# Low parts of two token tiles on GpSimd, and router and gather work at a higher priority, in a hybrid trunk layer with 32 experts

## The chip, the cores and the metric

The kernel runs on one core of one Trainium2 chip. The metric is the device time of one execution in microseconds (us), as the median of several runs.

## What is computed

One layer over 512 latent tokens of 1024 channels, with a context of 256 tokens. Three token mixers (centred pooling, differential attention, a bidirectional RWKV scan) are merged and projected back to 1024 channels, and the result is added to the tokens. Then comes a mixture of experts, which is what this case is about: each token chooses one of 4 groups and in it 2 of 8 experts. Cut to that part:

```python
lg  = h @ w_rg                                   # h: modulated RMSNorm of the tokens, 512 x 1024
grp = argmax(lg)                                 # 1 of 4 groups
le  = (h @ w_re) of that group                   # 8 experts of it
top_v, top_i = lax.top_k(le, 2)
gates = softmax(lg)[grp] * softmax(top_v)
eid   = grp * 8 + top_i                          # 32 experts in all
y_e   = (silu(xb @ w_g[e]) * (xb @ w_u[e])) @ w_d[e]     # 1024 -> 512 -> 1024, tokens of expert e
out   = x + mod[5] * sum over the two experts of gate * y_e
```

The weights of the 32 experts are 201 MB in fp32, and each is used once.

## The kernel before

**Stages.** The mixers and the merge take the first part of the execution. Then the output projection is made in four column blocks of 256, each for four token tiles of 128 (`out_mm` L1446 on TensorE, `out_add` L1452 to L1458 on VectorE and ScalarE). As soon as a tile has its last block, its routing begins. The experts follow, each for at most 64 tokens (a path for more is not taken here). The experts come in batches of four, whose tokens are gathered together.

**Routing of one tile t** (all of it stands between the last output products and the first expert). `turned` transposes the tile's tokens on TensorE (L1369), and ScalarE copies them (L1370). `logits` multiplies them by the router's weights (L1376, 8 products a tile, 32 in all). `route` (L1380 to L1401, all on VectorE but for one power on GpSimd, L104) scales them, takes the largest group and the two largest experts and writes one-hot rows. `count` (L1409, and L1410 on VectorE) numbers the tokens of every expert, which gives each token a slot. `normed` writes the normalised tokens twice over. The high part is a rounded copy (L1436, ScalarE, in two halves). The low part is what the rounding left out (L1437, VectorE, 128x1024). A plain copy (L1440, ScalarE) goes to memory (L1441). High and low part together are multiplied as two products where fp32 would be needed.

**Gathering the first batch.** `chosen` (L1500, VectorE) makes a 0/1 matrix of a tile's tokens against the 256 slots of four experts. `rows_of` (L1506, TensorE) multiplies high and low part by it, summed over the four tiles, and `put` (L1511 on ScalarE, L1513 on VectorE) writes the result to xT, the input of the first four experts. `slots` (L1484 to L1491) gathers the gates (`gates`, L1416 to L1427, put into `tgx` by L1601 to L1603). Later batches are fetched from the stored copy instead.

**Experts.** `up` (L1608) makes the first expert product from xT and the weights, `hidden` and `turn_` the activation, `down` (L1643) the second product, and `parts_of` (L1661, GpSimd) and `add` (L1653) bring it to the tokens. `load` (L1257) issues the weights' transfers on SyncE, 1 MB at a time, into a ring of 13 buffers (`ew`), and two more loads go into buffers that the stage needs later anyway (names `oh`, `yhl`, `xT`). Several of the ring's buffers lie where the mixers and the routing kept their data, so a load waits until those have been read. One of them (buffer 10) lies where the plain copies, named F, were.

**Order.** The code is written tile by tile, and a scheduler sets each engine's order by a priority that falls with the place in the code. `tc.high_priority(n)` moves what it encloses ahead by n places. Each engine then works through its list in order, and each instruction waits for the semaphores of what it needs. In names of the trace, `xn` is the tokens' high and low parts, `oh` the 0/1 matrices, `F` transposed tokens and copies, `psm` and `pp` PSUM tiles.

Of the kernel before, what the change touches and what calls it, by code (L numbers as in the profile page):

```python
# [9 lines left out]
FT = mybir.dt.float32  # L10
# [68 lines left out]
def trunk_kernel(ctx: ExitStack, tc: tile.TileContext, I, out, dbg=None, upto=99):  # L79
# [65 lines left out]
    def ps_big(shape=(128, 512)):  # L145
        return ppool.tile(list(shape), FT, name="pp", bufs=5)
# [1282 lines left out]
    def normed(t):  # L1429

        if t % 2 == 0:
            xns.append(xnp.tile([128, 2, 2, D], FR, name=f"xn{t // 2}"))
        hi, lo = xns[t // 2][:, 0, t % 2], xns[t // 2][:, 1, t % 2]
        for h in range(2):
            sl = slice(h * 512, h * 512 + 512)
            S.activation(hi[:, sl], xt2[t][:, sl], AF.Copy, scale=ss[:, t, 3:4])  # L1436
        V.scalar_tensor_tensor(lo, xt2[t], ss[:, t, 3:4], hi.bitcast(FT), op0=OP.mult, op1=OP.subtract)  # L1437

        xf = wfa.tile([128, D], FT, name="F", bufs=7 - FB)
        S.activation(xf, xt2[t], AF.Copy, scale=ss[:, t, 3:4])  # L1440
        nc.scalar.dma_start(x_d[t * 128:(t + 1) * 128], xf)  # L1441

    def out_mm(p, w, t, k):
# [50 lines left out]
    def gather(b):  # L1494
# [20 lines left out]
        if b == 0:  # L1515

            ahead = {}
            for t in range(3):
                chosen(t)
                yield  # L1520
            for k in range(AH):
                ahead[k] = ps_big()[:, 0:EB * 64]
                rows_of(ahead[k], k, range(3))
            chosen(3)
            yield
            xT = ep.tile([128, KD, EB * 64], FT, name="xT")
            for k in range(KD):
                p = ahead[k] if k in ahead else ps_big()[:, 0:EB * 64]
                rows_of(p, k, (3,) if k in ahead else range(4))
                put(k, p)  # L1530
            yield xT, *slots(b, oh)
            return
        for t in range(4):
# [31 lines left out]
    for t in range(5):  # L1565
        if t < 4:
            p = ps_big()[:, 0:256]
            for k in range(KD):
                out_mm(p, wo[3], t, k)
            out_add(p, t, 3)  # L1570
        if t:
            with tc.high_priority(0):
                turned(t - 1, 4, 4)
                logits(t - 1, 0, 8)
                if t > 1:
                    count(t - 2)
                route(t - 1)
            normed(t - 1)
        if t > 1:
            next(nxt)  # L1580
# [340 lines left out]
```

## Time and profile before

| | |
|---|---|
| median of 3 runs (1440.27 to 1447.98) | 1447.19 us |
| the profiled execution | 1448.53 us |
| its span, first to last instruction | 1446.6 us |
| TensorE's mean granted clock | 0.977 |
| busy: TensorE, VectorE, ScalarE, GpSimd | 1362.2, 822.0, 482.5, 382.5 us |
| transfers | 399.96 MB, mean 276 GB/s |

Busy times are sums over the whole span, and TensorE's includes the time in which it works through products whose weights have just come. The span divides at about 970 us: before it are the mixers, the merge and the routing; behind it the experts, in which the transfers run at the same rate from slice to slice.

### The profile page before, as it was taken

The page shows a single profiled execution, that of the slowest core. Times are in us where ns is not written, and L with a number is a line of the kernel's source. Part 1 is how long each engine was busy: PE and PEld are TensorE (multiplying, and loading weights), DVE is VectorE, ACT ScalarE, POOL GpSimd, SP SyncE. Part 2 cuts the span into 40 slices and gives each one's busy share as a digit, 9 for nine tenths or more (in the row PEclk, how much of TensorE's full clock was granted, in tenths as well). Part 3 has the DMA queues.
Part 4 walks back from the last instruction along what each step waited for, and adds up shares of the span by engine and source line. Part 5 has one row for each costly group of instructions (what it writes and reads, how often), then busy time and mean ns, then how long its engine had stood idle before and what let it go on. Part 6 is the DMA issues. An engine that isn't in the chain of part 4 may idle for free.

```text
span 1446.6 us, 24032 instructions
## 1 busy us (share of the span) xinstructions
PE 1362.2 (94%) x9148; PEld 1018.7 (70%) x9148; DVE 822.0 (57%) x1673; ACT 482.5 (33%) x1089; POOL 382.5 (26%) x345
## 2 busy tenths in 40 slices
PE   5999999998999999799999998999999999999897
PEld 3786788887888888688887776985555554555443
DVE  4553327779988958266776886462433433333334
ACT  4432235665565632144445523341111111111101
POOL 2111155445432444112221257110101101111001
PEclk9999999999999999799999999999999999999999
DMA  9368755666566466965847276579999999999996
GB/s 367 151 216 309 236 181 171 215 210 199 193 217 217 179 206 214 252 209 159 260 136 240 85 259 234 204 277 417 419 418 418 419 419 419 419 418 419 419 419 241
DMA packets 138038, 399.96 MB, mean 276 GB/s; under 512 B 38757, under 2 KB 69477, under 8 KB 107200
## 3 DMA queue, kind: packets, MB, share of 16 engines
q1 hardware_dynamic: 101920, 331.55, 61.9%
q10 hardware_dynamic: 32400, 58.60, 11.1%
q0 software_dynamic: 3600, 8.24, 1.7%
q8 instruction: 74, 1.21, 0.3%
q14 instruction: 44, 0.36, 0.1%
HBM read 343.44 MB, written 58.72 MB: 278 GB/s over the span
## 4 chain that ended last, share of the span: by engine, by line
PE 42%; DMA 25%; DVE 8%; issue 3%; ACT 2%; POOL 1%; SPq 1%; ACTq 0%; DVEq 0%; POOLq 0%
DMA ew<-in_w_eu_dram 9%; DMA ew<-in_w_ed_dram 5%; PE pp L220 5%; PE pp L1608 5%; DMA ew<-in_w_eg_dram 4%; PE pp L1152 3%; PE pp L1446 3%; PE pp L1643 2%; PE pp L234 2%; PE sc L1007 2%; PE pp L825 1%; PE pp L812 1%; PE sc L1006 1%; DMA F<-in_w_eg_dram 1%; PE pp L818 1%
## 5 line engine op out<-in xcount | busy, mean ns | idle before, releaser
L1608 PE MATMUL pp<-ew,xT 128*64 128x256 f32 x1888 | 225.0, 383 | 14.4 <-DMA ew<-in_w_eu_dram 9.4
L1608 PEld LDWEIGHTS pp<-ew,xT 128*64 128x64 f32 x1888 | 132.0, 137 | 97.4 <-issue 18.5
L220 PE MATMUL pp<-xlh,wh 128*128 128x512 f32 x344 | 135.7, 405 | 1.3 <-ACT wide L413 1.3
L220 PE MATMUL pp<-xll,wh 128*128 128x512 f32 x344 | 135.7, 395 | 0.4 <-POOL xll L320 0.4
L220 PE MATMUL pp<-xlh,wl 128*128 128x512 f32 x344 | 135.1, 393 | 0.0
L1661 POOL TENSOR_TENSOR yhl<-m,yhl 128x512 fp32r<-128x512 f32 x30 | 38.2, 1272 | 364.0 <-ACT yhl L1660 364.0
L215 POOL TENSOR_TENSOR wl<-wraw,wh 128x512 fp32r<-128x512 f32 x84 | 113.4, 1377 | 64.1 <-ACT wh L214 59.9
L1653 DVE TENSOR_TENSOR x<-x,pp 128x512 f32<-128x512 f32 x128 | 80.7, 681 | 41.6 <-PE pp L1652 41.5
L1643 PE MATMUL pp<-ew,hT 128*64 128x512 f32 x440 | 101.0, 599 | 0.0
L1614 DVE TENSOR_TENSOR hh<-hh,pp 128x256 f32<-128x256 f32 x32 | 13.5, 421 | 148.1 <-ACT hh L1613 148.1
L1646 DVE SCALAR_TENSOR_TENSOR m<-pp,gc,m 64x512 f32<-64x512 f32 x62 | 46.5, 750 | 63.3 <-PE pp L1643 62.6
L220 PEld LDWEIGHTS pp<-xlh,wh 128*128 128x128 f32 x344 | 64.7, 190 | 20.8 <-issue 5.6
L214 ACT ACTIVATE wh<-wraw 128x512 fp32r<-128x512 f32 (+1 forms) x112 | 61.1, 612 | 54.1 <-PE pp L220 51.7
L220 PEld LDWEIGHTS pp<-xll,wh 128*128 128x128 f32 x344 | 65.2, 190 | 15.1 <-issue 2.0
L220 PEld LDWEIGHTS pp<-xlh,wl 128*128 128x128 f32 x344 | 65.2, 189 | 13.8
L1643 PEld LDWEIGHTS pp<-ew,hT 128*64 128x64 f32 x440 | 29.0, 136 | 55.9 <-issue 50.9
L234 PE MATMUL pp<-wh,xlh 128*128 128x256 f32 x192 | 59.5, 310 | 5.1 <-ACT qo L659 2.3
L806 POOL TENSOR_TENSOR ao<-ar,cst 128x512 f32<-128x512 f32 x24 | 30.8, 1284 | 124.3 <-PE pp L818 68.3
L1622 ACT ACTIVATE hT<-psm 128x256 f32<-128x256 f32 x32 | 12.3, 384 | 149.7 <-PE psm L1620 144.2
L1613 ACT ACTIVATE hh<-pp 128x256 f32<-128x256 f32 x32 | 12.3, 384 | 139.9 <-PE pp L1608 139.9
L234 PE MATMUL pp<-wl,xlh 128*128 128x256 f32 x192 | 57.7, 300 | 0.0
L234 PE MATMUL pp<-wh,xll 128*128 128x256 f32 x192 | 57.5, 299 | 0.0
(436 smaller groups left out, 3133.4 us busy)
## 6 DMA issues: line engine op xcount, KB each, us to landing
ew<-in_w_eg_dram SPq DMA_DIRECT2D x59, 1024.0 KB
ew<-in_w_eu_dram SPq DMA_DIRECT2D x58, 1024.0 KB
ew<-in_w_ed_dram SPq DMA_DIRECT2D x56, 1024.0 KB
wraw<-in_w_in_dram SPq DMA_DIRECT2D x27, 1024.0 KB
u_d<-ub ACTq DMA_DIRECT2D x16, 1152.0 KB
wada<-in_w_adr_dram SPq DMA_DIRECT2D x16, 1024.0 KB
ar<-u_d SPq DMA_DIRECT2D x24, 640.0 KB
wa<-in_w_ad_dram SPq DMA_DIRECT2D x8, 1024.0 KB
```

The lines of the kernel that those rows point to most:

```text
L214: S.activation(self.h[:, kk, :n], raw[:, kk, :n], AF.Copy)
L215: (eng[q % 2] if type(eng) is tuple else eng).tensor_sub(self.l[:, kk, :n], raw[:, kk, :n], self.h[:, kk, :n].bitcast(FT))
L220: PE.matmul(ps, a[:, k, cs], b[part][:, k], start=(k + n == 0), stop=(k == KD - 1 and n == 2))
L234: PE.matmul(ps, a[part][:, k, ts], b[:, k], start=(n == 0), stop=(n == 3 * KD - 1))
L806: G.tensor_mul(ao, aa[:, :, 2:3].to_broadcast([128, 4, 2, 64]), offm[:, None].to_broadcast([128, 4, 2, 64]))
L1152: PE.matmul(ps, a[:, k], bs[k][:, x], start=(c == 0), stop=(c == 11))
L1446: PE.matmul(p, a[:, ts], x[:, k], start=(k == 0 and c == 0), stop=(k == KD - 1 and c == 2))
L1608: PE.matmul(pg[64 * h:64 * h + 64, i], xT[:, k], of(w[i], k)[:, h * 256:h * 256 + 256], start=(k == 0), stop=(k == KD - 1), tile_position= ...
L1643: PE.matmul(pd[64 * h:64 * h + 64], hT[:, k], of(w[2], k)[:, h * 512:h * 512 + 512], start=(k == 0), stop=(k == 3), tile_position=(0, 64 * h))
L1646: V.scalar_tensor_tensor(y[ps_, h * 512:h * 512 + 512], pd[64 * h:64 * h + 64], gc, m5[ps_, h * 512:h * 512 + 512], op0=OP.mult, op1=OP.mult)
L1653: V.tensor_add(xt2[t][:, sl], xt2[t][:, sl], p)
L1661: eng.tensor_sub(yl, y[:, sl], yh.bitcast(FT))
```

## The change

Three things are edited. For the last two tiles (t > 1) the low part is no longer computed by VectorE from the tokens, but by GpSimd from ScalarE's plain copy, in two halves of 512; ScalarE's copy has thus one reader more than the store. The last matrix `chosen(3)` and the loop that makes xT are at priority 200. The block of `turned`, `logits`, `count` and `route` in the last output loop goes from priority 0 to 100.

```diff
@@ normed
-        V.scalar_tensor_tensor(lo, xt2[t], ss[:, t, 3:4], hi.bitcast(FT), op0=OP.mult, op1=OP.subtract)
+        if t < 2:
+            V.scalar_tensor_tensor(lo, xt2[t], ss[:, t, 3:4], hi.bitcast(FT), op0=OP.mult, op1=OP.subtract)
 
         xf = wfa.tile([128, D], FT, name="F", bufs=7 - FB)
         S.activation(xf, xt2[t], AF.Copy, scale=ss[:, t, 3:4])
+        if t > 1:
+            for h in range(2):
+                sl = slice(h * 512, h * 512 + 512)
+                G.tensor_sub(lo[:, sl], xf[:, sl], hi[:, sl].bitcast(FT))
@@ gather, first batch
-            chosen(3)
+            with tc.high_priority(200):
+                chosen(3)
             yield
             xT = ep.tile([128, KD, EB * 64], FT, name="xT")
-            for k in range(KD):
-                p = ahead[k] if k in ahead else ps_big()[:, 0:EB * 64]
-                rows_of(p, k, (3,) if k in ahead else range(4))
-                put(k, p)
+            with tc.high_priority(200):
+                for k in range(KD):
+                    p = ahead[k] if k in ahead else ps_big()[:, 0:EB * 64]
+                    rows_of(p, k, (3,) if k in ahead else range(4))
+                    put(k, p)
@@ the last output loop
-            with tc.high_priority(0):
+            with tc.high_priority(100):
                 turned(t - 1, 4, 4)
                 logits(t - 1, 0, 8)
```

Lines behind the edit move by 5 to 7: L1446 becomes L1451, L1500 L1505, L1506 L1511, L1484 L1489, L1601 L1608, L1608 L1615.

TensorE's list from the last output product (L1446) on, before:

```order
L1446 MATMUL pp<-xn_8964,ew_8462 128x256
L1376 MATMUL pp<-wg__8936,F 128x36 x8
L1409 MATMUL psm<-rt,cst 128x32
L1369 MATMUL psm<-cst,x_8918 128x128 x8
L1376 MATMUL pp<-wg__8936,F 128x36 x8
L1506 MATMUL pp<-oh,xn_9480 128x256 x6
L1409 MATMUL psm<-rt,cst 128x32 x2
L1506 MATMUL pp<-oh,xn_9480 128x256 x14
L1409 MATMUL psm<-rt,cst 128x32 x7
L1506 MATMUL pp<-oh,xn_9623 128x256 x20
L1484 MATMUL psm<-tgx,oh 128x6 x8
```

And after, where `xn_9480` holds tiles 0 and 1 and `xn_9623` tiles 2 and 3:

```order
L1451 MATMUL pp<-xn_8964,ew_8462 128x256
L1376 MATMUL pp<-wg__8936,F 128x36 x4
L1409 MATMUL psm<-rt,cst 128x32
L1369 MATMUL psm<-cst,x_8918 128x128 x8
L1511 MATMUL pp<-oh,xn_9480 128x256 x6
L1376 MATMUL pp<-wg__8936,F 128x36 x8
L1511 MATMUL pp<-oh,xn_9480 128x256 x2
L1409 MATMUL psm<-rt,cst 128x32 x2
L1511 MATMUL pp<-oh,xn_9480 128x256 x12
L1409 MATMUL psm<-rt,cst 128x32 x7
L1511 MATMUL pp<-oh,xn_9623 128x256 x10
```

Behind the last output product stand 12 router products (L1376) instead of 16, the first four of them tile 1's second half, and the last tile's eight now stand behind the first six gather products.

VectorE's list around the matrix of token tile 2 (the first of the two L1500, which takes its slots from the L1410 before it), before:

```order
L1422 TENSOR_SCALAR gv<-gv 128x4
L1401 TENSOR_TENSOR rt<-oo 128x32
L1423 RECIPROCAL gv<-gv 128x4
L1410 SCALAR_TENSOR_TENSOR slot<-psm,rt 128x32
L1424 TENSOR_TENSOR gv<-gv 128x4
L1500 TENSOR_TENSOR oh<-slot,cst 128x256
L1425 TENSOR_TENSOR gv<-gv 128x4
L1426 TENSOR_TENSOR oo<-oo,gv 128x256
L1410 SCALAR_TENSOR_TENSOR slot<-psm,rt 128x32
L1427 TENSOR_TENSOR tg<-oo 128x128
L1500 TENSOR_TENSOR oh<-slot,cst 128x256
L1601 CAST tgx<-cst 128x64x2
```

And after (L1505 is the matrix, L1608 to L1610 write tgx):

```order
L1422 TENSOR_SCALAR gv<-gv 128x4
L1401 TENSOR_TENSOR rt<-oo 128x32
L1423 RECIPROCAL gv<-gv 128x4
L1424 TENSOR_TENSOR gv<-gv 128x4
L1425 TENSOR_TENSOR gv<-gv 128x4
L1426 TENSOR_TENSOR oo<-oo,gv 128x256
L1427 TENSOR_TENSOR tg<-oo 128x128
L1410 SCALAR_TENSOR_TENSOR slot<-psm,rt 128x32
L1608 CAST tgx<-cst 128x64x2
L1609 CAST tgx<-tg 128x64x2
L1505 TENSOR_TENSOR oh<-slot,cst 128x256
L1610 TENSOR_TENSOR tgx<-tg,tgx 128x64x2
```

The gates' last three instructions and two of the three that write tgx now stand ahead of tile 2's matrix.

GpSimd's list at the same place (L104 is the power of a tile, L1701 and L1708 the same clearing in the expert stage), before:

```order
L1328 TENSOR_TENSOR xn_8951<-F,xn_8951 128x512
L1328 TENSOR_TENSOR xn_8964<-F,xn_8964 128x512
L104 TENSOR_TENSOR ss<-ss,nhalf 128x1 x4
L1701 MEMSET xn_9820 128x2048
L1701 MEMSET xn_9821 128x2048
```

And after:

```order
L1328 TENSOR_TENSOR xn_8951<-F,xn_8951 128x512
L1328 TENSOR_TENSOR xn_8964<-F,xn_8964 128x512
L104 TENSOR_TENSOR ss<-ss,nhalf 128x1 x3
L1445 TENSOR_TENSOR xn_9623<-F,xn_9623 128x512 x2
L104 TENSOR_TENSOR ss<-ss,nhalf 128x1
L1445 TENSOR_TENSOR xn_9623<-F,xn_9623 128x512 x2
L1708 MEMSET xn_9822 128x2048
```

The two subtractions of tile 2 stand between the powers of tiles 2 and 3, and those of tile 3 behind the last power.

SyncE's next loads behind the output products, with what each waits for, before:

```order
L1257 DMA ew_9716<-in_w_eu_dram 128x2048 [waits DMAHW2_49,PE_49]
L1257 DMA ew_9738<-in_w_eu_dram 128x2048 [waits DMAHW4_49,DMAHW5_49,DMAHW1_49,Activation_49]
L1257 DMA ew_9740<-in_w_ed_dram 128x2048 [waits DMAHW6_49,PE_49]
L1257 DMA oh<-in_w_ed_dram 128x1024 [waits DMAHW7_49,DVE_49]
L1257 DMA yhl<-in_w_ed_dram 128x1024 [waits DMAHW0_49,Activation_49]
```

And after:

```order
L1257 DMA ew_9718<-in_w_eu_dram 128x2048 [waits DMAHW2_49,PE_49]
L1257 DMA ew_9740<-in_w_eu_dram 128x2048 [waits DMAHW1_49,DMAHW5_49,PE_49,Pool_49]
L1257 DMA ew_9742<-in_w_ed_dram 128x2048 [waits DMAHW6_49,PE_49,Activation_49]
L1257 DMA oh<-in_w_ed_dram 128x1024 [waits DMAHW7_49,DVE_49]
L1257 DMA yhl<-in_w_ed_dram 128x1024 [waits DMAHW0_49,Activation_49]
```

The second of them is the load into buffer 10. DMAHW4, which is the queue of the last tile's store (L1441), is no longer among its waits, and GpSimd is.

## Rows read from the trace of the kernel before

**Rows 1.** Page, slices: GB/s moved in each of 40 equal slices of the span.

```profile
GB/s 367 151 216 309 236 181 171 215 210 199 193 217 217 179 206 214 252 209 159 260 136 240 85 259 234 204 277 417 419 418 418 419 419 419 419 418 419 419 419 241
```

**Rows 2.** SyncE's timeline, 948 to 975 us: start, duration, engine, line, tiles, count.

```profile
950.96 10.73 SPq L1257 DMA_DIRECT2D ew<-in_w_eu_dram  x2
...
962.32 0.33 SPq L1257 DMA_DIRECT2D oh<-in_w_ed_dram  x1
...
963.43 0.43 SPq L1257 DMA_DIRECT2D xT<-in_w_ed_dram  x1
970.90 0.34 SPq L1257 DMA_DIRECT2D ew<-in_w_ed_dram  x1
```

**Rows 3.** Windows: us; PE, PEld, DVE, ACT, POOL busy; PEclk, DMA share, GB/s.

```profile
957.00:960.00 3.00, 2.73 (x19) 2.15 (x19) 2.97 (x26) 0.35 (x2) 0.00 (x0) 1.00 0.72 291
960.00:963.00 3.00, 2.72 (x24) 2.60 (x24) 2.75 (x15) 0.07 (x1) 0.00 (x0) 1.00 0.29 49
```

**Rows 4.** TensorE's timeline, 950 to 972 us; in brackets the idle time before.

```profile
950.76 1.87 PE L1376 MATMUL pp<-wg__8936,F 128*128 128x36 f32 x16
...
958.23 1.45 PE L1506 MATMUL pp<-oh,xn 128*128 128x256 f32 x10 [0.23 <-DVE oh L1500]
...
961.70 2.63 PE L1506 MATMUL pp<-oh,xn 128*128 128x256 f32 x20
...
968.92 3.24 PE L1608 MATMUL pp<-ew,xT 128*64 128x256 f32 x28
```

**Rows 5.** VectorE's timeline, 949 to 963 us.

```profile
949.82 0.26 DVE L1385 SCALAR_TENSOR_TENSOR lgs<-pp,ss,lb 128x36 f32<-128x36 f32 x1 [0.63 <-PE pp L1376]
...
952.41 1.29 DVE L1437 SCALAR_TENSOR_TENSOR xn<-x,ss,xn 128x1024 fp32r<-128x1024 f32 x1 [0.16 <-ACT xn L1436]
...
957.75 0.42 DVE L1500 TENSOR_TENSOR oh<-slot,cst 128x256 fp32r<-128x256 f32 x1
...
960.76 0.43 DVE L1500 TENSOR_TENSOR oh<-slot,cst 128x256 fp32r<-128x256 f32 x1
...
961.30 0.43 DVE L1426 TENSOR_TENSOR oo<-oo,gv 128x256 f32<-128x256 f32 x1
...
962.01 0.28 DVE L1427 TENSOR_TENSOR tg<-oo 128x128 f32<-128x128 f32 x1
```

**Rows 6.** Timelines of ScalarE and GpSimd, 950 to 957 us.

```profile
950.96 0.72 ACT L1436 ACTIVATE xn<-x,ss 128x512 fp32r<-128x512 f32 x1 [1.30 <-PE pp L1446]
...
954.50 1.33 ACT L1436 ACTIVATE xn<-x,ss 128x512 fp32r<-128x512 f32 x2
955.75 1.14 ACT L1440 ACTIVATE F<-x,ss 128x1024 f32<-128x1024 f32 x1
...
953.92 0.56 POOL L104 TENSOR_TENSOR ss<-ss,nhalf 128x1 f32<-128x1 f32 x1 [5.44 <-DVE ss L1380]
```

**Rows 7.** Page, costliest groups: count | busy us, mean ns | idle before.

```profile
L1661 POOL TENSOR_TENSOR yhl<-m,yhl 128x512 fp32r<-128x512 f32 x30 | 38.2, 1272 | 364.0 <-ACT yhl L1660 364.0
```

**Rows 8.** Timelines of GpSimd and VectorE, 910 to 915 us.

```profile
910.60 3.24 POOL L1328 TENSOR_TENSOR xn<-F,xn 128x512 fp32r<-128x512 f32 x2 [3.19 <-ACT xn L1327]
...
910.52 0.68 DVE L1328 TENSOR_TENSOR xn<-F,xn 128x512 fp32r<-128x512 f32 x1
911.21 1.48 DVE L1353 TENSOR_TENSOR wg__8936<-wr,g2c 128x288 f32<-128x288 f32 x1
912.61 0.41 DVE L1452 TENSOR_TENSOR tm<-pp,m 128x256 f32<-128x256 f32 x1
912.94 1.45 DVE L1328 TENSOR_TENSOR xn<-F,xn 128x512 fp32r<-128x512 f32 x1
```

**Rows 9.** TensorE's timeline and one window, 879 to 888 us.

```profile
879.53 0.39 PE L1152 MATMUL pp<-bs,mwl 128*128 128x512 f32 x1
...
883.63 1.22 PE L1152 MATMUL pp<-F,mwh 128*128 128x512 f32 x2 [3.26 <-ACT mwh L1144]
...
880.50:887.30 6.80, 3.26 (x7) 2.16 (x8) 3.50 (x5) 1.78 (x3) 6.80 (x5) 0.66 0.40 123
```

## The prediction

> **What bounds the kernel now.** I read the page's slices first. From slice 28 on the transfers run flat at 417 to 419 GB/s until slice 39 [rows 1]: that is the expert stage, and there the weights that still have to come decide the end. All that the change touches lies before it, between the last output products and the first expert product, 951 to 969 us. So the question is not how busy TensorE is but when the steady stream of weights can start, and whether it can go on.
>
> SyncE's own timeline shows what starts it [rows 2]. One load of 1 MB goes out at 951, and the second of its row only where the row ends, near 961.3; with that one, and up to the load into xT at 963.43, 4 MB are asked for between 961.3 and 963.9 (another of 1 MB, two of 0.5 and the last of 1). The next load can only follow when the first expert's first products have freed a buffer: it is issued at 970.90. At 418 GB/s a load of 1.05 MB takes 2.5 us, so the 4 MB that start near 962.3 last until about 972.3; the release at 970.90 comes 1.4 us before the stream would run dry. From there on every load is tied to a buffer that TensorE frees. Before, the transfers had idle time: shares of 0.72 and 0.29 in the two slices from 957 to 963 [rows 3], together 0.28 x 3 + 0.71 x 3 = 3.0 us.
>
> TensorE's timeline gives the other side [rows 4]. After the last output product, which releases ScalarE at 950.96 [rows 6], it works through a queue in order: router products, counts, the products that gather the first batch. It waits little (0.23 us at 958.23 for a selection matrix), and 7.2 us after it has the matrix of token tile 2 (961.70) it starts the first expert (968.92). What it waits for comes from VectorE, whose timeline is packed from 949.8 to 962.3 [rows 5]: the routing of tiles 1, 2 and 3 interleaved, with two low-part instructions L1437 of 1.29 us among them (the one at 952.41 stands for both), and the selection matrices L1500 at 957.75 (tile 1) and 960.76 (tile 2). So the chain that sets the first expert product is VectorE's.
>
> **The change part by part.** Tile numbers are 0 to 3.
>
> *Router products.* The priorities move eight instructions of this kind, and not all upward: 20 of the 32 now stand ahead of the last output product instead of 16, but tile 1's second four stand right behind it. Sixteen executed instructions, eight products, take 1.87 us [rows 4], 0.23 each, so four more put the last output product 0.9 us later, at 951.8. That is work moved, not added: the queue behind it is 0.9 us shorter. Tile 1's logits, read by VectorE at 949.82 before, come at 952.6 at the earliest: 2.8 us later.
>
> *Low parts leave VectorE.* Two instructions of 1.29 us go, 2.6 us. Both stood ahead of tile 1's selection matrix. Against that, tile 1's routing, much of which ran under the last output products, now starts 2.8 us later. The two about cancel: with nothing else, that matrix would be ready where it was, near 958.2.
>
> *Low parts on GpSimd.* Four subtractions of 128x512 at 1.27 us [rows 7]. The high part of tile 2 can't be written before the last output product, since its buffer held output weights: ScalarE was released by TensorE at 950.96 [rows 6]. Now 951.8; its halves of 0.7 us are there at 952.5 and 953.1, so the first pair of subtractions runs from 952.5 to 955.1. Tile 3's power (0.56 us at 953.92 before) is queued behind them, and behind the power wait tile 3's high part, its copy, the copy's store and the two exponentials of the gates on ScalarE. In rows, the power moves from 953.92 to 955.7, the high part from 954.50 to 956.3, the copy from 955.75 to 957.6, and the second pair of subtractions then takes 958.6 to 961.2 or so.
>
> *What the subtractions do to VectorE.* This is the term that decides. At 910.60 GpSimd runs two subtractions of this form in 3.24 us, and VectorE beside them [rows 8]: the 128x512 subtraction at 910.52, which had started first, takes 0.68 us; the 128x288 product that starts at 911.21 takes 1.48 us, and the 128x512 one at 912.94 takes 1.45 us, while the instruction between them that reads PSUM takes its usual 0.41. The held ones end 0.4 to 0.6 us after a GpSimd instruction ends: they waited for it and then ran. So an instruction of VectorE with two operands in SBUF waits for the whole subtraction, and a second one waits for the next. [...]
>
> Going through VectorE's new list with these times: during the first pair tile 0's selection matrix wants to start at 953.2 and gets in at 953.9 (0.7), and tile 3's scale L1380 wants 954.5 and gets 955.6 (1.0). During the second pair the mask L1392 wants 958.7 and gets 959.9 (1.2), and the gates' difference L1416 wants 960.3 and gets 961.3 (1.0). Together 3.9 us; the bounds are 0 (all slips between) and 4 x 1.27 = 5.1. I take 3.9, since the list there is nearly all such instructions. Tile 1's matrix is then ready at 962.1 instead of 958.2.
>
> *Order on VectorE.* Between the matrices of tiles 1 and 2 lay 3.0 us (957.75 to 960.76). The new list puts five more ahead of tile 2's: L1425, L1426 (0.43), L1427 (0.28) and the two casts into tgx, some 1.3 us at these rows, and takes two small ones away, 0.3: 4.0 us. Tile 2's matrix ends at 961.19 + 3.9 + 1.0 = 966.1.
>
> *First expert product.* TensorE's 7.2 us behind that matrix are the same products in another order: 966.2 + 7.2 = 973.4, less than 0.1 for the wait that goes, so 4.5 us later than 968.92. The higher priority of the first batch's inputs changes no count there; it only puts the last of the eight products for gates and slots behind tile 3's gather products, cost 0, since both are before the first expert product.
>
> *The stream.* One load (buffer 10) no longer waits for the store of tile 3's copy, by the waits listed with SyncE's order; it and its follower can go near 957 and fill most of the 3.0 us of idle transfer time. But the next ones wait for L1427 (issued at 962.32, right after its end at 962.29), which moves to near 965.5, and the first release moves from 970.90 to 975.4. All that was asked for has landed before that, so the early loads only lengthen the gap. The stream goes on at 975.4 instead of 972.3 at best (+3.1) and 4.5 later at worst. I take the middle, **+3.8 us**. The tail behind the last landing is the same.
>
> Sum: the profiled execution took 1448.53 us (span 1446.6 and 1.9 around it), so 1452.3. The median of the runs is 1.3 lower: 1447.19 + 3.8 = 1451.0.
>
> **The rivals.**
> 1. *The hold doesn't bite* (chance 0.22). Small instructions slip in, as one of each kind does beside a subtraction that it preceded [rows 8]. Then only the order is left: tile 2's matrix +1.0, first product +1.0, the stream between -0.4 (971.9 against the 972.3 at which it would run dry) and +1.0: about 1447.5. Against it: 1.48 for 0.4 us of work.
> 2. *The earlier loads pay: faster* (0.10). If tile 2's matrix is ready before 961.2, the release holds its place and buffers 10 and 11 fill the idle 3.0 us: 1447.19 - 3.0 = 1444.2. More isn't there, since TensorE waits under 1 us in its queue. For it: the removed 2.6 us. Against it: tile 1's routing moved behind the last output product.
> 3. *TensorE's clock falls: slower beyond the forecast* (0.15). [...]
>
> **How the numbers follow.** Forecast 0.53: 1451.0, its own range +2 to +5.5, 1449 to 1453. Range for 8 in 10: down to rival 2 less a little scatter (one of the three runs was 1440.27), up to rival 3 and the bound of 5.1 us of holds: 1442 to 1457. 0.5% is 7.2 us, about what a measurement of this kernel can tell from no change: below 1440.0 only scatter leads, 0.05; above 1454.4 most of rival 3 and a little of the forecast, 0.19; the rest, 0.76.
>
> **What would show it.** In the new trace: GpSimd's four subtractions of 1.3 us or more near 952 and 958, with VectorE instructions of over 1 us beside them (L1380, L1392, L1416, a matrix); tile 3's power behind 955; a TensorE wait of over 2 us before tile 1's gather products; the first expert product near 973; SyncE's load of buffer 10 near 957 and a gap in the transfers before 975. If the first expert product stands at 969 or before, or VectorE's small instructions keep their 0.2 us, the forecast's term is wrong; if the end doesn't follow the first expert product, the reading of the stream is.

## The result, and where the time went

The changed kernel takes 1455.54 us (median of 5 runs, 1454.42 to 1456.86) against 1444.86 us for the kernel before in the same comparison (5 runs, 1440.27 to 1447.98). The ratio is 1.0072 with a 95% interval of 1.0054 to 1.0089: 10.7 us slower.

TensorE's timeline of the changed kernel, from the last output product on (columns as in [rows 4]; L1505 is the selection matrix, L1511 the gather products, L1615 the first expert product; the first row, the counts of tile 1, is needed further down):

```profile
955.66 0.53 PE L1409 MATMUL psm<-rt,cst 128*128 128x32 f32 x4
...
960.05 0.85 PE L1409 MATMUL psm<-rt,cst 128*128 128x32 f32 x6 [1.50 <-DVE rt L1401]
962.29 1.43 PE L1409 MATMUL psm<-rt,cst 128*128 128x32 f32 x8 [1.39 <-DVE slot L1410]
963.54 2.48 PE L1511 MATMUL pp<-oh,xn 128*128 128x256 f32 x10
...
971.22 5.45 PE L1511 MATMUL pp<-oh,xn 128*128 128x256 f32 x24
976.59 3.24 PE L1615 MATMUL pp<-ew,xT 128*64 128x256 f32 x28
```

The waits are the numbers in brackets: 1.50 us for tile 2's one-hot rows and 1.39 us for its slots. Before, TensorE didn't wait for those rows at all, and for the slots it waited 0.28 us, as this line of the same timeline shows:

```profile
960.79 1.08 PE L1409 MATMUL psm<-rt,cst 128*128 128x32 f32 x8 [0.28 <-DVE slot L1410]
```

But the larger loss lies behind them. The ten gather products at 963.54 take 2.48 us, 0.25 each; before, ten took 1.45 [rows 4, at 958.23]. From 963.54 to the first expert product TensorE works without a break for 13.05 us, where it needed 7.22 before (961.70 to 968.92), for the same products. The window of that stretch gives the reason (columns as in [rows 3]):

```profile
963.50:976.00 12.50, 12.50 (x60) 12.50 (x60) 3.58 (x11) 1.69 (x3) 0.10 (x1) 0.50 0.56 218
```

TensorE is busy all the time, 12.5 of 12.5 us, at a granted clock of 0.50. In the kernel before the whole stretch ran at 1.00 ([rows 3] up to 963, and here the rest):

```profile
963.00:966.00 3.00, 3.00 (x29) 3.00 (x28) 2.15 (x7) 1.04 (x2) 0.00 (x0) 1.00 0.93 382
966.00:969.00 3.00, 3.00 (x27) 2.87 (x28) 0.91 (x3) 0.57 (x1) 0.37 (x1) 1.00 0.98 393
```

VectorE and GpSimd beside each other show where the waits come from:

```profile
951.22 1.17 DVE L1505 TENSOR_TENSOR oh<-slot,cst 128x256 fp32r<-128x256 f32 x1
...
952.46 1.09 DVE L1380 SCALAR_TENSOR_TENSOR ss<-ss 128x1 f32<-128x1 f32 x1
...
957.06 1.15 DVE L1392 TENSOR_SCALAR sm<-cst,sm 128x4 f32<-128x4 f32 x1
...
958.41 1.02 DVE L1398 CAST sm<-i 128x2 f32<-128x2 uint32 x1
...
961.84 0.29 DVE L1427 TENSOR_TENSOR tg<-oo 128x128 f32<-128x128 f32 x1
962.05 0.18 DVE L1410 SCALAR_TENSOR_TENSOR slot<-psm,rt 128x32 f32<-128x32 f32 x1
...
962.42 0.42 DVE L1505 TENSOR_TENSOR oh<-slot,cst 128x256 fp32r<-128x256 f32 x1
```

```profile
950.82 2.70 POOL L1445 TENSOR_TENSOR xn<-F,xn 128x512 fp32r<-128x512 f32 x2 [3.29 <-ACT xn L1436]
...
956.65 2.75 POOL L1445 TENSOR_TENSOR xn<-F,xn 128x512 fp32r<-128x512 f32 x2 [2.49 <-ACT F L1441]
```

Four instructions of VectorE last over 1 us, and all of them start while GpSimd subtracts: the matrix of tile 0 (1.17 us, 0.42 when it is free), L1380 (1.09, of 0.15), L1392 (1.15, of 0.23) and L1398 (1.02, of 0.17). In sum they were held 3.5 us. The last three lines show the order: the gates (L1427 is their last instruction) pass ahead of tile 2's slots (L1410, 962.05) and matrix (962.42).

SyncE then shows the end of the chain, to be read against [rows 2]:

```profile
949.95 8.65 SPq L1257 DMA_DIRECT2D ew<-in_w_eu_dram  x2
958.73 0.57 SPq L1257 DMA_DIRECT2D ew<-in_w_ed_dram  x1
...
978.58 0.34 SPq L1257 DMA_DIRECT2D ew<-in_w_ed_dram  x1
```

Its windows at 972 and at 981 us:

```profile
972.00:978.00 6.00, 6.00 (x36) 5.37 (x37) 0.73 (x2) 1.84 (x4) 2.10 (x2) 0.62 0.01 4
981.00:982.00 1.00, 1.00 (x12) 0.80 (x11) 0.00 (x0) 0.00 (x0) 0.00 (x0) 1.00 0.95 401
```

The load that waited for the last tile's store does start earlier (the row at 949.95 ends at 958.60, and the next one is issued at 958.73), so everything asked for has landed by 972. Then the transfers stand still for 6 us (share 0.01) until the first release at 978.58, and they are back at 0.95 only from 981 on. From that release to the end of the span it takes 476.5 us, where it took 475.7 before.

The stages before the output projection vary by some microseconds from one execution to the next, so spans of single profiles can't be compared directly. Counted from the first output product (895.18 before, 893.37 after) the loss is:

| stretch | before | after | difference |
|---|---|---|---|
| first to last output product | 55.78 | 56.58 | +0.8 |
| last output product to tile 2's gather | 10.74 | 13.59 | +2.9 |
| tile 2's gather to the first expert product | 7.22 | 13.05 | +5.8 |
| first expert product to the end | 477.7 | 478.5 | +0.8 |

Together +10.3 us, close to the 10.7 of the medians. "Last output product" is read here and below as the moment at which its release starts a load on SyncE (950.96 and 949.95).

### The profile page after: what moved, and what is told of

It is laid out like the page before. It is cut to its first block, busy times and chain, and to the rows that moved or that the text cites. A ratio compares the mean times of both kernels' runs of the same rounds, so it can differ in the third digit from the quotient of the medians.

```text
span 1455.1 us, 24038 instructions
## 1 busy us (share of the span) xinstructions
PE 1366.3 (94%) x9148; PEld 1022.4 (70%) x9148; DVE 822.8 (57%) x1671; ACT 482.7 (33%) x1089; POOL 388.2 (27%) x349
## 4 chain that ended last, share of the span: by engine, by line
PE 51%; DMA 16%; DVE 8%; issue 3%; ACT 2%; POOL 1%; SPq 1%; ACTq 0%; DVEq 0%; POOLq 0%
PE pp L1615 9%; DMA ew<-in_w_eu_dram 8%; PE pp L220 5%; PE pp L1650 5%; PE pp L1152 4%; PE pp L1451 3%; PE pp L1658 2%; PE pp L234 2%; PE sc L1007 2%; PE pp L825 2%; PE pp L837 2%; PE sc L1006 1%; DMA ew<-in_w_eg_dram 1%; PE pp L1659 1%; PE pp L812 1%
## 5 line engine op out<-in xcount | busy, mean ns | idle before, releaser
L1615 PE MATMUL pp<-ew,xT 128*64 128x256 f32 x1888 | 225.4, 383 | 14.8 <-DMA ew<-in_w_eu_dram 10.0
L1615 PEld LDWEIGHTS pp<-ew,xT 128*64 128x64 f32 x1888 | 132.2, 137 | 97.8 <-issue 18.2
```

The lines of the kernel that those rows point to most:

```text
L1615: PE.matmul(pg[64 * h:64 * h + 64, i], xT[:, k], of(w[i], k)[:, h * 256:h * 256 + 256], start=(k == 0), stop=(k == KD - 1), tile_position= ...
```

## The experiments

The theory after reading the two traces: GpSimd's subtractions hold VectorE, TensorE waits for it, and the waits bring TensorE's clock down, which costs more than the waits. The main rivals: the order that the priorities make costs the time by itself; and the clock falls for a reason that has nothing to do with the waits. For each kernel the table gives the interval from the last output product to the first expert product in its profile, and the ratio of its time to that of the kernel before. The interval is one profile's; the ratio also holds what the earlier stages vary by, and the two agree to within 3 us. The clock of a stretch is likewise read from one execution of each kernel.

| kernel | interval, us | ratio (95%) |
|---|---|---|
| before, two profiles | 17.96, 17.96 | 1 |
| changed, two profiles | 26.64, 27.30 | 1.0072 (1.0054 to 1.0089) |
| priorities only | 23.02 | 1.0045 (1.0025 to 1.0066) |
| GpSimd only | 20.95 | 1.0030 (1.0007 to 1.0054) |
| clear, not subtract | 23.56 | 1.0045 (1.0027 to 1.0063) |
| changed, waits filled | 23.36 | 1.0056 (1.0032 to 1.0079) |
| changed, filled elsewhere | 27.12 | 1.0050 (1.0032 to 1.0068) |
| priorities, filled | 22.86 | 1.0023 (1.0009 to 1.0037) |
| before, wait added | 23.60 | 1.0030 (1.0017 to 1.0043) |
| before, low parts late | 24.64 | 1.0027 (1.0011 to 1.0043) |
| priorities, low parts late | 20.13 | one run |
| the same, filled | 22.48 | 1.0030 (1.0011 to 1.0050) |

**Both kernels once more.** No edit; a second profile of each.

> The kernel before, unchanged, profiled once more. If its interval from the last output product to the first expert product is a property of the kernel: 17.5 to 18.5 us, granted clock 1.00 over the gather products, waits of under 0.4 us on TensorE there. If the first profile was a lucky one: a stretch at 0.50 and 20 us or more.

The kernel before repeats itself: 945.07 to 963.03 us, 17.96 as the first time, no wait over 0.28 us and the clock at 1.00 throughout. Its timeline and window:

```profile
954.89 1.08 PE L1409 MATMUL psm<-rt,cst 128*128 128x32 f32 x8 [0.28 <-DVE slot L1410]
```

```profile
955.80:963.00 7.20, 7.20 (x62) 7.10 (x61) 4.16 (x16) 1.61 (x3) 0.25 (x1) 1.00 0.91 335
```

> The changed kernel, profiled once more. If the fall of the clock belongs to it: 0.50 from the counts of tiles 2 and 3 to the first expert product, interval 25.5 to 27.5 us. If it comes and goes: a profile with 1.00 there and an interval of 20 to 21 us.

The changed kernel has the fall again (947.87 to 975.17, 27.30 us), but at another place:

```profile
953.63 0.90 PE L1409 MATMUL psm<-rt,cst 128*128 128x32 f32 x4
...
957.39 2.50 PE L1511 MATMUL pp<-oh,xn 128*128 128x256 f32 x10 [2.27 <-DVE oh L1505]
```

```profile
955.00:957.40 2.40, 0.12 (x2) 0.01 (x1) 2.40 (x5) 0.00 (x0) 2.06 (x2) 0.50 1.01 358
```

```profile
955.87 1.47 DVE L1505 TENSOR_TENSOR oh<-slot,cst 128x256 fp32r<-128x256 f32 x1
```

The counts of tile 1 already take 0.90 us, where the first profile had 0.53 (955.66): the clock falls near 953.5, behind waits of only 0.57 and 0.18 us, at which the first profile kept 1.00 (0.58 and 0.19). The second pair of subtractions starts 6.70 us behind the last output product, as in the first profile, but the slow counts have made tile 1's slots 0.3 us late (6.70 against 6.41 us). So this time the matrix of tile 1 falls into the subtractions and is held, 1.47 us, and TensorE waits 2.27 us for it. Here that long wait comes behind the fall and can't be its cause. So the fall belongs to the kernel, not to one profile, but the two waits of 1.50 and 1.39 us aren't what it needs.

**The two halves of the change.** First the priorities alone, with all four low parts on VectorE as before:

```diff
-            with tc.high_priority(0):
+            with tc.high_priority(100):
                 turned(t - 1, 4, 4)
...
+            with tc.high_priority(200):
+                chosen(3)
```

> The priorities as in the changed kernel, but VectorE computes all four low parts as before; no GpSimd subtraction. Theory (the subtractions hold VectorE, TensorE then waits about 3 us in sum near 957 to 963 and its clock falls): VectorE's holds (0.75, 0.94, 0.92 and 0.85 us, 3.5 in sum) go and two low parts of 1.2 us come back, so tile 2's matrix is about 1 us earlier than in the changed kernel; TensorE's waits there shrink to about 2 us, the granted clock stays 1.00, the first expert product stands near 970 and the time is within 2 us of the kernel before. Rival (the order does it: tile 1's router products behind the last output product, the gates ahead of tile 2's matrix): the clock falls to 0.50 here as well, the first expert product stands at 975 or later and the time is 6 to 11 us above the kernel before.

```profile
955.23 1.59 PE L1506 MATMUL pp<-oh,xn 128*128 128x256 f32 x10 [1.52 <-DVE oh L1500]
...
958.71 0.56 PE L1484 MATMUL psm<-tgx,oh 128*128 128x6 f32 x2 [0.76 <-DVE slot L1410]
```

```profile
957.00:966.00 9.00, 8.24 (x39) 8.13 (x39) 3.26 (x13) 0.00 (x0) 0.00 (x0) 0.50 0.99 390
```

The theory expected the clock to hold, and it fell: TensorE waits 1.52 us for tile 1's matrix, and the clock is 0.50 from 957 to 966; the wait of 0.76 us for tile 2's slots lies inside that stretch. The interval is 23.0 us, 5.1 over the kernel before, with no instruction of GpSimd in sight. So the holds are not needed for the fall. By the lists the order makes the waits: tile 1's second router products come behind the last output product, and the gates pass ahead of tile 2's slots. The rival's number (975 or later, counted where the profile of before has 950.96) wasn't reached either: 970.43 here is 974.0 on that scale. Its time was reached: the ratio makes 6.5 us, within the rival's 6 to 11.

Then the low parts on GpSimd at the old priorities:

```diff
...
+        if t > 1:
+            for h in range(2):
+                sl = slice(h * 512, h * 512 + 512)
+                G.tensor_sub(lo[:, sl], xf[:, sl], hi[:, sl].bitcast(FT))
```

> The low parts of tiles 2 and 3 on GpSimd, at the priorities of the kernel before. Theory: VectorE is held four times, 3 to 4 us in sum, and spared 2.6, so tile 2's matrix ends about 1 us later than before (962 instead of 961.2); TensorE's waits sum to 1.5 to 3 us between 957 and 963. If they reach what they are in the changed kernel (two of about 1.4 us) the clock falls and the time is 5 to 9 us above the kernel before; if not, it is 0 to 2 us above. Rival (the order does it): clock 1.00, the first expert product within 1 us of 969, no difference in time.

```profile
951.23 0.63 PE L1409 MATMUL psm<-rt,cst 128*128 128x32 f32 x4 [0.93 <-DVE rt L1401]
...
959.02 1.08 PE L1409 MATMUL psm<-rt,cst 128*128 128x32 f32 x8 [0.28 <-DVE slot L1410]
959.93 4.05 PE L1511 MATMUL pp<-oh,xn 128*128 128x256 f32 x20
```

```profile
953.30:957.00 3.70, 3.70 (x21) 3.70 (x21) 2.96 (x17) 0.69 (x2) 2.54 (x2) 0.57 0.69 281
960.00:963.70 3.70, 3.70 (x21) 3.70 (x21) 2.37 (x8) 0.67 (x2) 0.00 (x0) 0.59 1.01 421
```

A wait of 0.93 us that ends at 951.23, and the clock is at 0.57 and 0.59 in two stretches, with 0.96 from 957 to 960 between them; the twenty gather products at 959.93 take 4.05 us against 2.63 [rows 4, at 961.70]. The interval is 3.0 us longer, and the time 4.3 us, between the two cases of the theory. Its runs scatter from 1441.94 to 1456.93, more than those of any other kernel here. The second fall comes behind waits of 0.23 and 0.28 us only, at which the kernel before kept its clock; so the last wait alone doesn't decide.

**No subtraction, the rest unchanged.** GpSimd clears the four half low parts, so tiles 2 and 3 are gathered without their low parts:

```diff
-                G.tensor_sub(lo[:, sl], xf[:, sl], hi[:, sl].bitcast(FT))
+                G.memset(lo[:, sl].bitcast(FT), 0.0)
```

> As the changed kernel, but GpSimd clears the four half low parts instead of subtracting, so tiles 2 and 3 are gathered without their low parts: an instruction of the same tile in the same place that reads nothing from SBUF. Theory: VectorE's instructions beside it keep their 0.15 to 0.43 us, tile 2's matrix ends near 959.5 to 960, TensorE waits under 1 us in a piece, clock 1.00, the first expert product at 967 to 969, time 3 us below to 1 us above the kernel before. Rival (GpSimd's work holds VectorE whatever it reads, or the holds don't matter): instructions of over 0.9 us on VectorE as in the changed kernel, or none and the clock at 0.50 all the same; the time 8 to 11 us above the kernel before.

```profile
948.93 1.92 POOL L1445 MEMSET xn<- 128x512 f32 x4 [2.51 <-PE pp L1451]
```

```profile
950.11 0.42 DVE L1505 TENSOR_TENSOR oh<-slot,cst 128x256 fp32r<-128x256 f32 x1
...
957.80 0.29 DVE L1427 TENSOR_TENSOR tg<-oo 128x128 f32<-128x128 f32 x1
958.01 0.18 DVE L1410 SCALAR_TENSOR_TENSOR slot<-psm,rt 128x32 f32<-128x32 f32 x1
```

```profile
958.25 1.92 PE L1409 MATMUL psm<-rt,cst 128*128 128x32 f32 x8 [1.36 <-DVE slot L1410]
```

The hold is gone: beside the clearing, which by its row reads no tile, the matrix takes 0.42 us; beside a subtraction, which reads F and xn, it took 1.17 in the changed kernel. But the clearing waits for no copy of ScalarE's, so all four run by 950.85, tile 3's too: the later instructions of VectorE have nothing beside them. The interval is 3.1 us shorter than in the changed kernel: that is about what the subtractions cost, by their holds and their later place together. It is still 5.6 us over the kernel before. VectorE's lines show the order's part: L1426, L1427 and the small ones ahead of them run from 956.73 to 958.0, then L1410, and TensorE waits 1.36 us for it. The eight small products of that row take 1.92 us, where 1.08 was usual: the clock has fallen all the same, as the rival had said, and from 959.98 to the first expert product at 972.40 it is 12.42 us instead of 7.22, 5.2 of the 5.6. The time lies between what the theory (near the kernel before) and its rival (no gain) had said: the holds are one part, the order another.

**A wait alone.** The kernel before, its priorities and its engines, with tile 2's matrix written six times over:

```diff
             for t in range(3):
-                chosen(t)
+                for i in range((1, 1, 6)[t]):
+                    chosen(t)
                 yield
```

> The kernel before, with tile 2's selection matrix written six times over on VectorE instead of once (5 x 0.42 = 2.1 us more), nothing else changed: TensorE waits some 2 us longer for it, ahead of tile 2's gather products. Theory (a wait there brings the clock down): granted clock 0.50 behind the wait, gather products at 0.24 us instead of 0.12, interval 18.0 + 2.1 + 2 to 5 = 22 to 25 us, time 4 to 7 us above the kernel before. Rival (a wait costs only itself): clock 1.00, interval 20 us, time at most 2 us above.

```profile
956.61 0.42 PE L1484 MATMUL psm<-tgx,oh 128*128 128x6 f32 x2 [2.38 <-DVE tgx L1604]
...
958.60 4.61 PE L1506 MATMUL pp<-oh,xn 128*128 128x256 f32 x20
```

```profile
956.60:963.00 6.40, 6.39 (x30) 6.40 (x31) 1.67 (x5) 0.74 (x2) 0.00 (x0) 0.51 1.00 405
```

This is the clearest of the runs. One wait of 2.38 us was put in, and the clock behind it is 0.51 for the next 6 us: twenty gather products take 4.61 us instead of 2.63. One more thing changed: the scheduler now puts two executions of L1484 and eight small products of L1745 (128x32) ahead of these, and it is the first of them that waits, for tgx. The clock falls within 0.3 us of the wait's end, before L1745 begins. The interval is 5.6 us longer: the wait ends 2.5 us later than the gather began before, and from there to the first expert product it takes 10.3 us instead of 7.2, which are the 3.1 that the clock adds.

**The waits filled.** The reverse, in the changed kernel: ten products that nobody needs, five ahead of the counts of tile 2 and five ahead of those of tile 3.

```diff
         pc = pl["c"][:, NE * t:NE * t + NE]
+        for i in range((0, 0, 5, 5)[t]):
+            PE.matmul(pl["c"][:, 256:512], K("ones"), cst[:, 0:256], start=True, stop=True)
```

> As the changed kernel, with ten more products on TensorE (128x256, five ahead of the counts of tile 2 and five ahead of those of tile 3, into unused columns of PSUM), which fill its waits there. VectorE is held as before. Theory (the fall of the clock costs 5.8 of the 7.7 us by which the first expert product is late): the granted clock stays 1.00, gather products take 0.12 us each instead of 0.24, the first expert product stands at 970.5 to 972.5, and the time is 2 to 5 us above the kernel before. Rival (the clock falls for another reason, or the loss is VectorE's lateness alone): clock 0.50 from 963 on and 8 to 12 us above the kernel before.

```profile
949.66 0.90 PE L1411 MATMUL psm<-rt,cst 128*128 128x32 f32 x4
...
956.94 2.43 PE L1409 MATMUL psm<-cst 128*128 128x256 f32 x10 [0.93 <-DVE slot L1412]
...
960.02 1.44 PE L1513 MATMUL pp<-oh,xn 128*128 128x256 f32 x10
```

```profile
956.90:967.20 10.30, 10.26 (x78) 9.89 (x78) 3.96 (x14) 1.59 (x3) 0.32 (x1) 1.00 0.77 292
```

What the clock costs is confirmed: at 1.00 the way from tile 2's gather (960.02) to the first expert product (967.23) takes 7.21 us, as in the kernel before (7.22), against 13.05 in the changed one. That filled waits keep the clock up is not shown. The counts of tile 1 take 0.90 us here too: the clock is 0.50 from about 949.5 to 952.7, behind waits of 0.57 and 0.18 us and ahead of the first filling products, and is back before the second ones. These stand behind a wait of 0.93 us and not in it, and the clock holds all the same. The interval falls from 26.64 to 23.36 us, though the filling products cost time of their own on the path: five of them (ten executions) take 2.43 us where only 0.4 us was left to wait, since tile 2's matrix is ready at 957.3. The time is 8.1 us above the kernel before by the ratio, not the 2 to 5 of the theory, and not clear of the changed kernel's. The profile is that of the fastest of the five runs (1447.49 us, the others 1450.04 to 1454.04), so it need not speak for them.

Three more kernels were filled at other places, two of them here. In the changed kernel and in the one with the priorities alone, eleven products behind tile 1's matrix, into a PSUM tile of their own:

```diff
...
+        if t == 2:
+            pl["f"] = ps_sm()[:, 0:EB * 64]
+        for i in range((0, 0, 8, 3)[t]):
+            PE.matmul(pl["f"], xns[0][:, 0, 1, 0:128], pl["o"][:, 1].rearrange("p e s -> p (e s)"), start=True, stop=True)
```

> As the changed kernel, with eleven more products on TensorE (128x256, some 0.14 us each, 1.6 in all) into a PSUM tile that nothing else uses or reads, right behind tile 1's matrix, so that they lie in its first two waits (0.59 and 1.50 us) and hold up nobody. From the last output product to the first expert product the kernel before took 18.0 us, the changed one 26.7. Theory (5.9 of the 8.7 us are the lower clock, and the clock falls because TensorE waits): granted clock 1.00 over the gather products, that interval 20 to 22 us, time 4 to 7 us under the changed kernel's. Rival (the clock falls whatever fills the waits): clock 0.50 behind the counts again, interval 25 us or more.

```profile
959.34 0.56 PE L1493 MATMUL psm<-tgx,oh 128*128 128x6 f32 x2 [1.98 <-DVE slot L1414]
```

> As the run with the priorities alone (no work on GpSimd), with the same eleven products in TensorE's waits. That run's interval from the last output product to the first expert product was 23.0 us with the clock at 0.50 for some 9 us of it. Theory: clock 1.00, interval 18.5 to 20 us (the order alone costs 1 to 2 us against 18.0), time 3 to 5 us under that run's and 0 to 3 above the kernel before. Rival (the order itself costs the 5 us, by work moved behind the last output product): interval 22 us or more at full clock.

```profile
956.34 2.69 PE L1411 MATMUL psm<-oh,xn 128*128 128x256 f32 x11 [1.36 <-DVE sm L1398]
```

```profile
961.00:965.00 4.00, 4.00 (x35) 4.00 (x35) 1.60 (x6) 0.00 (x0) 0.00 (x0) 0.93 0.98 389
965.50:968.00 2.50, 2.50 (x13) 2.50 (x14) 1.29 (x3) 1.13 (x2) 0.00 (x0) 0.50 1.05 437
```

Neither did what was meant. In the first the filling products lie ahead of the counts, a wait of 1.98 us remains behind them, and the fall comes there (27.12 us, the rival's 25 or more). In the second the clock falls at 954.4, behind a wait of 0.33 us and even ahead of the one of 1.36, so the filling products run at the lower clock themselves, 2.69 us for eleven (22.86 us). It is back at 961 and falls once more at 964.6, and there TensorE had not waited since 956.34: it was busy for 4.00 of 4.00 us with small products and gather products. So this second fall has no wait ahead of it, and the rival that the clock falls for another reason than the waits isn't ruled out.

**Shorter chains on VectorE.** Is there an order that beats both kernels? First the kernel before, with the low parts of tiles 2 and 3 pinned behind tile 2's matrix:

```diff
...
+                c_ = chosen(t)
+                if t == 2:
+                    with tc.issue_after(c_.ins):
+                        low(2)
+                        low(3)
```

> The kernel before at its own priorities, VectorE computing the low parts of tiles 2 and 3 right behind tile 2's selection matrix instead of ahead of tile 1's; no GpSimd. If the lateness of VectorE's chain sets the first expert product and no wait is added: tile 2's matrix is up to 2.5 us earlier, the gather of tile 2 starts 0 to 1.5 us earlier (its low part comes 1.3 us behind the matrix), the interval is 16.5 to 18 us and the time 0 to 2 us under the kernel before. If the two low parts then keep TensorE waiting for over 1 us and the clock falls: interval 20 to 23 us and 2 to 5 us above.

```profile
953.89 0.74 PE L1511 MATMUL pp<-oh,xn 128*128 128x256 f32 x4 [0.43 <-DVE lgs L1385]
...
955.97 2.63 PE L1511 MATMUL pp<-oh,xn 128*128 128x256 f32 x10 [0.74 <-DVE oh L1505]
```

Tile 2's gather does start earlier, 9.4 us behind the last output product instead of 10.7, but with waits of 0.43 and 0.74 us before it, and its ten products already take 2.63 us: the clock is low from there on, and the interval is 24.6 us, more than the 20 to 23 that a fall was to make of it. Then the same with the new priorities and the high-part products of tile 2 ahead of its low-part ones, without and with eleven filling products (the second diff):

```diff
...
-                rows_of(ahead[k], k, range(3))
+                rows_of(ahead[k], k, range(2))
+            for a in range(2):
+                for k in range(AH):
+                    rows_of(ahead[k], k, (2,), (a,))
```

```diff
...
+        for i in range((0, 8, 3, 0)[t]):
+            PE.matmul(pl["f"], xns[0][:, 0, 0, 0:128], pl["o"][:, 0].rearrange("p e s -> p (e s)"), start=True, stop=True)
```

> The priorities of the changed kernel, no work on GpSimd; VectorE's low parts of tiles 2 and 3 pinned behind tile 2's selection matrix, and the high-part products of tile 2 ahead of its low-part ones. VectorE's chain is up to 2.5 us shorter than with the priorities alone. If lateness and not waiting decides: interval 17 to 18.5 us. If any wait of some 0.7 us and more among TensorE's small products brings the clock down (as in the runs so far): 0.50 for 6 us and more, interval 19.5 to 23 us.

> As the run before it (priorities, low parts late, high parts first), with eleven more products on TensorE behind tile 0's matrix, ahead of the last router products, into a PSUM tile that nothing reads. If filled waits keep the clock: 1.00 throughout, the load of buffer 10 early, interval 17 to 19 us and the time from 3 us under the kernel before to 1 above. If the waits come behind the filling products, at tile 1's or tile 2's matrix: clock 0.50 all the same, interval 20 us or more, 3 to 6 us above the kernel before.

```profile
959.27 1.91 PE L1409 MATMUL psm<-rt,cst 128*128 128x32 f32 x8 [1.36 <-DVE slot L1410]
```

```profile
960.88 1.45 PE L1517 MATMUL pp<-oh,xn 128*128 128x256 f32 x10 [0.97 <-DVE oh L1511]
...
964.64 5.47 PE L1517 MATMUL pp<-oh,xn 128*128 128x256 f32 x24
```

Without the filling a wait of 1.36 us, again for the slots behind the gates, brings the clock down for 6 us (20.1 us). With it the clock holds until 963, through waits of 0.38 and 0.97 us, and falls then: the last 24 products take 5.47 us against 3.11. No version here beats the kernel before, whose TensorE waits under 0.3 us at a time.

## Why the prediction came out as it did

The direction was right, and the time lies in the range, near its upper end; the forecast of +3.8 us was too small by more than half. That the time lies inside is in part luck: the range was built on 1447.19 us for the kernel before, which came out at 1444.86 here, and the change of 10.7 us is more than the 9.8 from that base to the range's end. By its steps:

- **Where the end is decided** held. In all fourteen profiles of this case the span ends 475.4 to 476.7 us behind the first release, whatever the kernel. The early load came as foretold and gained nothing, also as foretold.
- **Router products**: four more of them put 0.8 us on the output loop (55.78 to 56.58), 0.9 was said. Tile 1's logits are read 0.8 us behind the last output product (950.77), as worked out.
- **The low parts' slots on GpSimd** were right to 0.2 us: 0.9 us behind the last output product (0.7 said) and 6.7 (6.8 said).
- **What the subtractions do to VectorE** was right in size, four holds and 3.5 us in sum for 3.9, three of the four instructions those named. The fourth was L1398 instead of L1416. That L1398, which reads a single tile of 128x2, is held too goes beyond what [rows 8] had shown.
- **Order on VectorE** was listed (+1.0), and that is where the first omission lies: it was counted as lateness alone. With the holds gone it still makes TensorE wait 1.36 us in a piece.
- **Tile 1's matrix** was to be ready 10.3 us behind the last output product (962.1 against 951.8), with all four holds ahead of it, and TensorE was to wait over 2 us for it. In the first profile two of the holds come behind it, it is ready after 7.1 us, and the wait is 0.59 us; in the second it is 9.5 and 2.27 us.
- **Tile 2's matrix** ends 12.9 us behind the last output product (14.0 in the second profile). The sum had 14.3, against 10.2 before. So far the working holds in its sum, and would have given a first expert product some 3 to 4 us late.
- **First expert product** is the step that failed: "TensorE's 7.2 us behind that matrix are the same products in another order". They are the same products, but at a clock of 0.50 they take 13.05 us. This is the term that was mis-sized: 0 was put down for the clock, 5.8 us was measured.
- **The stream**: the sum gave back 0.7 us for weights still on their way; 0.8 us was lost instead. Why is not shown. The transfers come back to their rate only some 2 us after the release, but so they do with the low parts late (a share of 0.07 from 969 to 972, the release at 973.21, 0.27 from 972 to 975 and 0.95 from 975 to 978), and there the end follows after 475.4 us, 0.3 less than before.

Rival 3 is thus what happened, with a chance of 0.15. The top of the range counts it in at a cost that was the author's estimate and that no run shows; the runs showed 5.8 us for the gather at 0.50 instead of 1.00. Nor does a run show how long a wait has to be: [rows 9] has one of 3.26 us behind which the clock was lower (0.66 in its window), and nothing of shorter ones. In the runs the clock fell behind single waits of 2.38, 1.52 and 1.36 us, behind 0.43 and 0.74 together, behind 0.57 and 0.18 in the changed kernel's second profile, and once behind none. In the changed kernel it was low for all of the gather of tile 2 and what follows, 0.50 over 12.50 us. Rival 1 said that without the holds the first expert product would be 1.0 us late; in the clearing kernel, without holds, the interval grew by 5.6. Rival 2 asked for tile 2's matrix no later than before; the changed kernel has it 2.7 us later, and two kernels with the low parts late, which had it earlier (9.3 and 9.8 us behind the last output product, against 10.2), had a clock of 0.50 around it.

How the loss divides is shown in part. With a clearing in the subtractions' place it is 3.1 us smaller (26.64 to 23.56), and without GpSimd altogether 3.6 smaller (23.02). Of the clearing kernel's rest of 5.6 us, 5.2 go with the clock. The two halves alone add 5.1 and 3.0 us to the interval, 8.1 in sum, and both together 8.7 and 9.3; since the fall of the clock is in every one of them, these are not parts of a whole. What stays open is what brings the clock down. One wait put into the kernel before was enough, and no profile of a changed order kept 1.00 throughout. But waits of 0.23 and 0.28 us went either way, so did waits of 0.57 and 0.18, and one fall had no wait ahead of it. Whether the small products have a part in it of their own, no run here tests.

## What to carry to other kernels

Before moving work in a stretch where TensorE runs small products one behind the other, list its waits there, and price each new one twice: for itself, and for the products behind it at a granted clock of 0.50, which lasted 3 to 20 us at a time here. An order that fills the engine's list just so was worth more here than a shorter list on the engine that feeds it: every version that took the two low parts off VectorE, or moved them, lost time. And count what an operation given to GpSimd costs VectorE beside it: here the four subtractions, which read two tiles each, held it for 3.5 us in sum, against 2.6 us of work taken away, while the clearings, which read none, left the matrix its 0.42 us.

## What the runs showed of the hardware that was not expected

- TensorE's granted clock fell to 0.50 behind waits much shorter than the 3.26 us in the trace of before [rows 9]: 1.36 us for one, 0.43 and 0.74 us for two. In the changed kernel waits of 0.57 and 0.18 us were followed by a fall in one profile and not in the other, and in the kernel with priorities and filling it fell a second time with no wait ahead (TensorE busy for 4.00 of 4.00 us). It stayed low for 3 to 20 us (from about 949.5 to 952.7 in the changed kernel with its waits filled, from near 953.5 to 974 in the second profile of the changed one), in the changed kernel's first profile although TensorE was then busy without a break (12.50 of 12.50 us in the window above).
- A VectorE instruction of 0.15 us on 128 single numbers (L1380) was held to 1.09 us beside a subtraction on GpSimd, as much as one of 128x256. Beside a clearing on GpSimd it took 0.16 us (950.62), and the matrix 0.42.
